# A given order for the first stage of a hybrid transformer layer: normalization, modulation and the first value projection

## The chip, the cores and the metric

The kernel runs on one core of a Trainium2 chip. The core has a matrix engine (PE), three engines for elementwise work (DVE, ACT, POOL), a queue engine that issues most of the loads and stores (SP), and 16 DMA engines that move the data. The metric is the device time of one execution in microseconds, as the median of several executions. A profile is one further execution with the hardware profiler on; its span is the time from the first to the last instruction.

## The reference

The reference is one layer of a diffusion transformer over 1024 latent tokens of width 1024, with 256 context tokens beside them. All is in float32. What matters here is its beginning:

```python
m_lat = silu(c) @ w_mod + b_mod          # 6 vectors of 1024: sh1, sc1, g1, sh2, sc2, g2
m_ctx = silu(c_ctx) @ w_mod + b_mod
h_lat = rms_norm(x, norm1_g) * (1.0 + sc1) + sh1
h_ctx = rms_norm(ctx, norm1_g) * (1.0 + csc1) + csh1
p_lat = h_lat @ w_in                     # 3584 columns: retention q, k, v, gate; attention q, k, v
p_ctx = h_ctx @ w_in
```

Behind it come a retention and a differential attention, an output projection with a gated residual, and a gated MLP with a convolution, also with a gated residual. The layer ends with a normalization.

## The kernel before

**Number format.** A float32 product is made of three products of a faster format: each operand is split into a high part (a rounded copy, on ACT) and a low part (the difference, on DVE or POOL). The function `passes` (L126) issues high times high (L129), high times low (L130) and low times high (L131) into one accumulator. Below, "product" is one such matmul with 512 columns; tile names with hi, or `hT` and `cT` as written on ACT, are high parts.

**First stage, L489 to L634.** `w_in` is cut into seven column groups of 512; the stage makes the first one, group 6 (the values of the attention), for the latent row tiles 0 to 5 of 128 rows each. The feature dimension of 1024 is cut into eight blocks of 128, called `d` or `k`. For each block the stage needs
- the modulation of this block: `mod_load` loads 128 x 2 columns of `w_mod` in two halves of 512 KB into one of five buffers `wt`; `mod_part` (L514) multiplies a half with the conditioning vectors, four small matmuls into `mods` (named `pr` in the profile); `mod_columns` (L519) copies the result to `rw` on ACT, sums it with two tiny matmuls into `pm` and writes the scale and shift columns `mcol` on DVE;
- the normalized rows: `normalize` (L528) takes the squares of a row tile on ACT, adds epsilon on DVE, takes the power -1/2 on POOL (L114 and L115) and scales the tile in place on DVE;
- the transposed and modulated block: `modulate` (L534) transposes four row tiles of 128 x 128 on PE into `pt`, applies scale and shift on ACT (high part, `hT`), does the same on DVE into `tmp`, and subtracts for the low part, on POOL where `d` is odd and on DVE where it is even. `pm` and `pt` share three banks;
- a slice of `w_in`, two blocks in a load of 512 KB (`raw`), split by ACT and DVE into `whi` and `wlo`.

`latents(0, d)` is `modulate` for row tiles 0 to 3, `latents(1, d)` for tiles 4 to 7. Row tiles 0 to 3 accumulate their products block by block in four banks (`part`) while the blocks are being made; the other half's normalization and transposes are spread between products by a generator (`second_rows`, through `beside` and `tick`), and so are the context rows (`ctx_rows`) between the products of row tiles 4 and 5. Row tiles 6 and 7 and the two context tiles follow at L649 and L650, then the other column groups.

**What sets the order.** The kernel is written against a scheduler that takes the instructions in the order of the program as a wish and gives each engine its order by its own estimate of when operands are ready. Each engine then executes strictly in that order. The function `in_order` (L117) takes a stretch of the program and chains the instructions of PE, DVE, ACT and SP to one another, so that the order written is the order executed; POOL is not chained. Before, it is used in the attention and at one place of the MLP.

Of the kernel before, what the change touches and what calls it, by code (L numbers as in the profile page):

```python
# [17 lines left out]
P = 128  # L18
# [54 lines left out]
def kernel(  # L73
# [39 lines left out]
    def rsqrt(out_ap, in_ap, mul, eps, n):  # L113
        nc.vector.tensor_scalar(out=out_ap, in0=in_ap, scalar1=mul, scalar2=eps, op0=ALU.mult, op1=ALU.add)  # L114
        nc.gpsimd.tensor_tensor(out=out_ap, in0=out_ap, in1=mhalf[:, :n], op=ALU.pow)  # L115
# [36 lines left out]
    with ExitStack() as p1:  # L152
# [344 lines left out]
        with ExitStack() as p0:  # L497
# [20 lines left out]

            def mod_columns(d):  # L519
                rw = xp.tile([P, 2 * P], F32, name="rw", bufs=2)  # L520
                nc.scalar.copy(rw, mods[:, d % 2])
                pm = pst.tile([P, 2, 2], F32, name="pm", tag="tr")
                for j in range(2):
                    mm(pm[:, j, :], rw[:, j * P : (j + 1) * P], fold, start=True, stop=True)
# [3 lines left out]
            def normalize(xt, col):  # L528
                sq = xp.tile([P, D], BF16, name="sq", bufs=1)
                nc.scalar.activation(sq, xt, AF.Square, accum_out=sm[:, col : col + 1])  # L530
                rsqrt(sm[:, col : col + 1], sm[:, col : col + 1], 1.0 / D, EPS, 1)
                nc.vector.tensor_scalar(out=xt, in0=xt, scalar1=sm[:, col : col + 1], scalar2=None, op0=ALU.mult)

# [12 lines left out]

            mods, wts = mm_tile("pr").rearrange("p (a b) -> p a b", a=2), {}
            wget, more = stream_parts(6)
            xc = []
            xs1 = [xp.tile([P, D], F32, name=f"xs1_{t}") for t in range(4)]  # L550

            def load_row(t):
# [4 lines left out]

            def part_products(t, k):
                passes(part[t], lat_lhs(t, k), wget(k, 0, 512), k == 0, k == KD - 1)
                tick()  # L560

            def second_rows():
                for t in range(4):
                    normalize(xs1[t], 6 + t)
                    yield
                for d in range(KD):
                    latents(1, d)
                    yield

            def ctx_rows():  # L570
                for t in range(NTC):
                    normalize(xc[t], t)
                    yield
                for d in range(KD):
                    modulate(xc, d, 1, cT[0][:, d, :], cT[1][:, d, :])
                    yield

            store = store_to(dv_row, c0=NTC)
            mod_load(0, 0)
            for t in range(3):  # L580
                load_row(t)
            mod_load(0, 1)
            load_row(3)
            more()
            for n in range(2, 5):
                mod_load(*divmod(n, 2))
            for q in range(2):
                mod_part(0, q)
            mod_load(2, 1)
            for t in range(4):  # L590
                normalize(xs0[t], 2 + t)
            mod_columns(0)
            latents(0, 0)
            for q in range(2):
                mod_part(1, q)
            mod_columns(1)
            latents(0, 1)
            more()
            part = [mm_tile("pn") for _ in range(4)]
            for k in range(KD):  # L600
                n = k + 2
                if k == 5:
                    beside(second_rows(), 0.9)
                if k == 6:
# [6 lines left out]
                if n + 1 < KD:  # L611
                    for q in range(2):
                        mod_load(n + 1, q)
                if k in (1, 2):
                    load_row(2 * k + 2)
                    load_row(2 * k + 3)
                if k in (1, 3):
                    more()
                part_products(0, k)
                if n < KD:  # L620
                    mod_part(n, 0)
                part_products(1, k)
                if n < KD:
                    mod_part(n, 1)
                part_products(2, k)
                if n < KD:
                    mod_columns(n)
                    latents(0, n)
                part_products(3, k)
            for t in range(4):  # L630
                store(t, part[t])
            beside(ctx_rows(), 0.7)
            natural(wget, lat_lhs, range(4, 6), store)
            beside(iter(()), 0.0)  # L634
        rc = late.enter_context(tc.tile_pool(name="rc", bufs=1))
# [817 lines left out]
```

## Time and profile before

| | |
|---|---|
| time, median of 3 executions | 1415.55 us (1414.84 to 1416.83) |
| profiled execution, its own time | 1411.45 us |
| its span | 1409.6 us |
| mean granted PE clock | 0.996 |
| PE, busy in the span | 97% |
| DVE, ACT, POOL, busy in the span | 70%, 52%, 20% |

The rows of the profile read as follows. A timeline row gives the start in the span, the duration, the engine, the line of the kernel, the operation with output and inputs, their shape, the count of instructions, and in brackets how long the engine stood idle before it and what ended that. Matmuls are pipelined, so one begins before the other ends: their pace is read from start to start, not from the duration. A float32 matmul counts as two instructions. A group of waits gives the total, the number and the longest.

### The profile page before, as it was taken

The page shows a single profiled execution, that of the slowest core. Times are in us where ns is not written, and L with a number is a line of the kernel's source. Part 1 is how long each engine was busy: PE and PEld are TensorE (multiplying, and loading weights), DVE is VectorE, ACT ScalarE, POOL GpSimd, SP SyncE. Part 2 cuts the span into 40 slices and gives each one's busy share as a digit, 9 for nine tenths or more (in the row PEclk, how much of TensorE's full clock was granted, in tenths as well). Part 3 has the DMA queues.
Part 4 walks back from the last instruction along what each step waited for, and adds up shares of the span by engine and source line. Part 5 has one row for each costly group of instructions (what it writes and reads, how often), then busy time and mean ns, then how long its engine had stood idle before and what let it go on. Part 6 is the DMA issues. An engine that isn't in the chain of part 4 may idle for free.

```text
span 1409.6 us, 19335 instructions
## 1 busy us (share of the span) xinstructions
PE 1365.5 (97%) x6988; PEld 1139.6 (81%) x6988; DVE 991.9 (70%) x1443; ACT 729.8 (52%) x1390; POOL 286.9 (20%) x321
## 2 busy tenths in 40 slices
PE   6899999999999999999999999999999999999996
PEld 3678888888887799998888778888888888788885
DVE  3564965333686798886457987777788877898457
ACT  3652312333575689997136645555455555455533
POOL 1320000000656133411201242233332220000001
PEclk9999999999999999999999999999999999999998
DMA  8535886365474697632321223223223226953224
GB/s 332 208 141 199 271 285 206 126 191 183 148 252 157 187 215 163 130 67 74 151 93 50 97 97 112 111 92 113 103 106 113 98 78 224 383 181 104 90 97 179
DMA packets 96663, 218.81 MB, mean 155 GB/s; under 512 B 9204, under 2 KB 31220, under 8 KB 96056
## 3 DMA queue, kind: packets, MB, share of 16 engines
q1 hardware_dynamic: 88408, 192.67, 39.6%
q0 software_dynamic: 8160, 24.91, 7.8%
q8 instruction: 55, 0.90, 0.3%
q14 instruction: 40, 0.33, 0.1%
HBM read 160.13 MB, written 57.41 MB: 154 GB/s over the span
## 4 chain that ended last, share of the span: by engine, by line
PE 79%; DMA 6%; issue 5%; DVE 5%; POOL 3%; ACT 2%; SPq 0%; POOLq 0%; DVEq 0%; ACTq 0%
PE chain L129 5%; PE pA L756 5%; PE chain L130 5%; PE pv L788 5%; PE chain L131 5%; PE c L131 4%; PE c L130 4%; PE c L129 4%; PE pn L130 4%; PE pn L131 3%; PE pn L129 3%; PE pl L131 3%; PE pl L129 3%; PE pl L130 3%; DMA W<-w_down 2%
## 5 line engine op out<-in xcount | busy, mean ns | idle before, releaser
L129 PE MATMUL chain<-T,whi 128*128 128x512 f32 x264 | 103.8, 394 | 5.0 <-ACT ua L1169 3.9
L129 PE MATMUL pl<-hT,whi 128*128 128x512 f32 x256 | 106.2, 415 | 0.0
L130 PE MATMUL chain<-T,whi 128*128 128x512 f32 x264 | 103.5, 392 | 0.0
L131 PE MATMUL chain<-T,wlo 128*128 128x512 f32 x264 | 103.1, 391 | 0.0
L131 PE MATMUL pl<-hT,wlo 128*128 128x512 f32 x256 | 100.2, 391 | 0.0
L130 PE MATMUL pl<-hT,whi 128*128 128x512 f32 x256 | 100.0, 391 | 0.0
L759 DVE TENSOR_REDUCE mt<-pA 128x1 f32<-128x1280 f32 x64 | 95.3, 1490 | 3.8 <-PE pA L756 2.7
L131 PE MATMUL c<-whi,ghl 128*128 128x512 f32 x232 | 90.4, 390 | 0.8 <-DVE ghl L1253 0.8
L756 PE MATMUL pA<-ks,qhl 128*128 128x512 f32 (+1 forms) x384 | 89.5, 369 | 1.0 <-ACT p L763 1.0
L130 PE MATMUL c<-wlo,ghl 128*128 128x512 f32 x232 | 90.3, 389 | 0.0
L129 PE MATMUL c<-whi,ghl 128*128 128x512 f32 x232 | 90.3, 389 | 0.0
L763 ACT ACTIVATE p<-pA,mt 128x1280 f32<-128x1280 f32 x64 | 85.5, 1336 | 6.5 <-DVE mt L759 6.5
L927 ACT CAST whi<-cmb 128x512 fp32r<-128x512 f32 x62 | 38.6, 623 | 85.1 <-PE chain L130 55.3
L129 PE MATMUL pn<-whi,hT 128*128 128x512 f32 x192 | 78.9, 412 | 1.3 <-ACT hT L541 1.0
L756 PEld LDWEIGHTS pA<-ks,qhl 128*128 128x128 f32 x384 | 67.6, 189 | 13.1 <-ACT p L763 1.7
L130 PE MATMUL pn<-wlo,hT 128*128 128x512 f32 x192 | 77.0, 401 | 0.4 <-DVE wlo L187 0.4
L1082 POOL TENSOR_TENSOR cmb<-wrb 128x512 f32<-128x512 f32 x20 | 26.4, 1322 | 249.3 <-DMA wrb<-w_up 90.4
L788 PE MATMUL pv<-va,aT 128*128 128x128 f32 x640 | 77.0, 276 | 0.1
L131 PE MATMUL pn<-whi,hT 128*128 128x512 f32 x192 | 75.7, 398 | 0.7 <-POOL hT L545 0.6
L788 PEld LDWEIGHTS pv<-va,aT 128*128 128x128 f32 x640 | 74.0, 192 | 1.0 <-DVE yT L817 0.6
L115 POOL TENSOR_TENSOR sm<-sm,mhalf 128x1 f32<-128x1 f32 x26 | 16.3, 626 | 286.2 <-DVE sm L114 286.1
L928 DVE TENSOR_TENSOR wlo<-cmb,whi 128x512 fp32r<-128x512 f32 x62 | 56.2, 908 | 21.7 <-ACT whi L927 21.3
(296 smaller groups left out, 3804.9 us busy)
## 6 DMA issues: line engine op xcount, KB each, us to landing
wm<-w_mod SPq DMA_DIRECT2D x32, 512.0 KB, 5.2
raw<-w_in SPq DMA_DIRECT2D x28, 512.0 KB, 5.1
wra<-w_up SPq DMA_DIRECT2D x24, 512.0 KB, 3.4
wrb<-w_up SPq DMA_DIRECT2D x23, 512.0 KB, 3.6
W<-w_down SPq DMA_DIRECT2D x44, 256.0 KB, 5.8
ad<-s SPq DMA_DIRECT2D x20, 512.0 KB, 3.5
wra<-ad SPq DMA_DIRECT2D x20, 512.0 KB, 3.3
kvs<-kvg SPq DMA_DIRECT2D x36, 256.0 KB, 3.0
```

Of the source, the lines that this page charges most:

```text
L115: nc.gpsimd.tensor_tensor(out=out_ap, in0=out_ap, in1=mhalf[:, :n], op=ALU.pow)
L129: mm(ps, lh, rh, start=first, stop=False, skip_group_check=more)
L130: mm(ps, lh, rl, start=False, stop=False, skip_group_check=more)
L131: mm(ps, ll, rh, start=False, stop=last, skip_group_check=more)
L756: mm(self.pa[m][:, c0:c1], self.q[:, m, i, qs], self.k[:, m, c0:c1], start=(i == 0), stop=(i == 1))
L759: nc.vector.tensor_reduce(out=self.mt[:, m : m + 1], in_=self.pa[m][:, :LK], axis=AX.X, op=ALU.min)
L763: nc.scalar.activation(self.p[m], self.pa[m][:, :LK], AF.Exp, scale=-1.0, bias=self.mt[:, m : m + 1], accum_out=self.s[:, m : m + 1])
L788: mm(self.pv, self.aT[:, c, :], self.v[:, c, :], start=(c == 0), stop=(c == NKT - 1))
L927: nc.scalar.copy(hi, src)
L928: nc.vector.tensor_tensor(out=lo, in0=src, in1=r32(hi), op=ALU.subtract)
L1082: nc.gpsimd.tensor_tensor(out=s1, in0=b1, in1=b2, op=ALU.add)
```

## The change

The stage is rewritten as one explicit sequence from the first load to the store of row tile 5, and `in_order` fixes it on PE, DVE, ACT and SP. Within it, the helper functions are cut into their steps (`mod_row` and `mod_sums` for `mod_columns`; `square`, `power` and `scale` for `normalize`), each of which has a place of its own. Each feature block has one batch of transposes, of sums and of modulation matmuls between its products. The first weight slice is loaded and split in two halves. Twenty matmuls of a tile of ones (`turn_over`) are added at the beginning; their result is overwritten. The generators are gone: squares and scaling of the second half stand in blocks 3 to 5, its transposes in blocks 6 and 7 and in row tile 4, and the context rows in row tiles 4 and 5. The diff, cut to what matters:

```diff
-            def mod_columns(d):
-                rw = xp.tile([P, 2 * P], F32, name="rw", bufs=2)
-                nc.scalar.copy(rw, mods[:, d % 2])
+            def mod_row(d):
+                rws[d] = xp.tile([P, 2 * P], F32, name="rw", bufs=2)
+                nc.scalar.copy(rws[d], mods[:, d % 2])
+            def mod_sums(d):
+                rw = rws.pop(d)
...
+            def scale(xt, col, c0=0, c1=D):
+                nc.vector.tensor_scalar(out=xt[:, c0:c1], in0=xt[:, c0:c1], scalar1=sm[:, col : col + 1], scalar2=None, op0=ALU.mult)
...
+            def part_products(ts, k):
+                for t in ts:
+                    passes(part[t], lat_lhs(t, k), wget(k, 0, 512), k == 0, k == KD - 1)
+            def turn_over(n):
+                for _ in range(n):
+                    mm(part[3][:, :P], ones, ones, start=True, stop=True)
...
+            turn_over(4)
+            mod_part(0, 0)
+            turn_over(10)
...
+            scale(xs0[3], 5, 0, 2 * P)
             latents(0, 0)
+            mod_part(1, 0)
+            mod_part(1, 1)
+            mod_row(1)
...
             for k in range(KD):
+                part_products((0, 1), k)
+                if k == 0:
+                    mod_sums(1)
+                    latents(0, 1)
+                if k < 2:
+                    for q in range(2):
+                        mod_part(k + 2, q)
+                    mod_row(k + 2)
+                if k == 7:
+                    latents(1, 2)
+                    latents(1, 3)
+                if 1 < k < 6:
+                    load_row(k + 2)
+                n = k + 4
+                if n < KD:
+                    for q in range(2):
+                        mod_load(n, q)
+                if k in (0, 2):
+                    w_load(2 + k // 2)
+                part_products((2, 3), k)
+                if k + 2 < KD:
+                    mod_sums(k + 2)
+                    latents(0, k + 2)
+                    if 0 < k < 5:
+                        for q in range(2):
+                            mod_part(k + 3, q)
+                        mod_row(k + 3)
+                if k in (0, 2, 4):
+                    w_split()
+                if k == 3:
+                    square(xs1[0], 6)
+                    power(6)
+                if k == 4:
+                    square(xs1[1], 7)
+                    scale(xs1[0], 6)
+                    power(7)
                 if k == 5:
...
+                    square(xs1[2], 8)
+                    scale(xs1[1], 7)
+                    power(8)
+                    square(xs1[3], 9)
+                    scale(xs1[2], 8)
+                    power(9)
+                    scale(xs1[3], 9)
+                if k >= 6:
+                    latents(1, 4 * (k - 6))
+                    latents(1, 4 * (k - 6) + 1)
...
+            def between(t, k):
+                if (t, k) == (4, 0):
+                    latents(1, 6)
+                    latents(1, 7)
...
+                if t == 5 and k % 2:
+                    context(k - 1)
+                    context(k)
...
+            in_order(begin)
```

How this moves the instructions is shown at three places. In the rows, `xs_172` to `xs_175` are the row tiles 0 to 3, and `xs_0` to `xs_3` with a number behind are the row tiles 4 to 7; `hT_168` and `hT_170` are high and low part of the first half, `hT_169` and `hT_171` of the second.

PE at the beginning of the program, before:

```order
L517 MATMUL pr<-wt,cz 32x256 x8
L524 MATMUL pm<-fold,rw 128x2 x2
L538 MATMUL pt<-ident,xs_172 128x128
L538 MATMUL pt<-ident,xs_173 128x128
L538 MATMUL pt<-ident,xs_174 128x128
L538 MATMUL pt<-ident,xs_175 128x128
L517 MATMUL pr<-wt,cz 32x256 x4
L129 MATMUL pn<-whi,hT_168 128x512
L130 MATMUL pn<-wlo,hT_168 128x512
```

and with the change:

```order
L590 MATMUL pn<-ones 128x128 x4
L517 MATMUL pr<-wt,cz 32x256 x4
L590 MATMUL pn<-ones 128x128 x10
L517 MATMUL pr<-wt,cz 32x256 x4
L590 MATMUL pn<-ones 128x128 x2
L527 MATMUL pm<-fold,rw 128x2 x2
L590 MATMUL pn<-ones 128x128 x4
L545 MATMUL pt<-ident,xs_172 128x128
```

The matmuls of ones (L590) fill the places between the first modulation matmuls, the sums and the transposes.

PE within feature block 1, before, from one half of a modulation batch to the products behind the transposes:

```order
L517 MATMUL pr<-wt,cz 32x256 x4
L130 MATMUL pn<-wlo,hT_168 128x512
L131 MATMUL pn<-whi,hT_170 128x512
L129 MATMUL pn<-whi,hT_168 128x512
L524 MATMUL pm<-fold,rw 128x2 x2
L538 MATMUL pt<-ident,xs_172 128x128
L538 MATMUL pt<-ident,xs_173 128x128
L538 MATMUL pt<-ident,xs_174 128x128
L538 MATMUL pt<-ident,xs_175 128x128
L130 MATMUL pn<-wlo,hT_168 128x512
```

and in a block with the change:

```order
L131 MATMUL pn<-whi,hT_170 128x512
L527 MATMUL pm<-fold,rw 128x2 x2
L545 MATMUL pt<-ident,xs_172 128x128
L545 MATMUL pt<-ident,xs_173 128x128
L545 MATMUL pt<-ident,xs_174 128x128
L545 MATMUL pt<-ident,xs_175 128x128
L517 MATMUL pr<-wt,cz 32x256 x8
L129 MATMUL pn<-whi,hT_168 128x512
```

The two halves of a modulation batch, which had products between them, now stand together behind the transposes.

ACT before, around the squares of the last two latent row tiles:

```order
L521 COPY rw<-pr 128x256
L530 ACTIVATE sq,sm<-xs_2_201 128x1024
L541 ACTIVATE hT_168<-pt,mcol 128x512
L530 ACTIVATE sq,sm<-xs_3_202 128x1024
L521 COPY rw<-pr 128x256
L186 CAST whi<-raw 128x1024
```

and with the change, at the end of block 5:

```order
L533 ACTIVATE sq,sm<-xs_1_204 128x1024
L548 ACTIVATE hT_168<-pt,mcol 128x512
L533 ACTIVATE sq,sm<-xs_2_205 128x1024
L533 ACTIVATE sq,sm<-xs_3_206 128x1024
L548 ACTIVATE hT_169<-pt,mcol 128x512 x4
L186 CAST whi<-raw 128x1024
```

The two squares stood ahead of the high parts of blocks 6 and 7 before; now they stand behind the first half's last high part (block 7), directly ahead of the second half's high parts.

POOL before, up to the context rows:

```order
L115 TENSOR_TENSOR sm<-sm,mhalf 128x1 x3
L545 TENSOR_TENSOR hT_170<-tmp,hT_168 128x512
L115 TENSOR_TENSOR sm<-sm,mhalf 128x1 x2
L545 TENSOR_TENSOR hT_170<-tmp,hT_168 128x512
L545 TENSOR_TENSOR hT_171<-tmp,hT_169 128x512
```

and with the change:

```order
L552 TENSOR_TENSOR hT_170<-tmp,hT_168 128x512 x3
L115 TENSOR_TENSOR sm<-sm,mhalf 128x1 x2
L552 TENSOR_TENSOR hT_170<-tmp,hT_168 128x512
L115 TENSOR_TENSOR sm<-sm,mhalf 128x1 x2
L552 TENSOR_TENSOR hT_171<-tmp,hT_169 128x512 x4
```

The powers (L115) of row tiles 6 and 7 are now behind the low part of block 7. Behind the stage the engines' rows are the same as before, except that on SP two loads and stores have changed places, and that a weight split of the next column group (ACT L186, DVE L187) stands within the transposes of the second half on ACT and DVE, in both versions.

More of the change, by code (lines that the diff above doesn't have):

```diff
@@ L545, in modulate, with wget, w_load, w_split @@
                 eng.tensor_tensor(out=lo, in0=tmp[:, :n], in1=r32(hi), op=ALU.subtract)
-            mods, wts = mm_tile("pr").rearrange("p (a b) -> p a b", a=2), {}
-            wget, more = stream_parts(6)
-            xc = []
+            mods, wts, rws = mm_tile("pr").rearrange("p (a b) -> p a b", a=2), {}, {}
+            part = [mm_tile("pn") for _ in range(4)]
+            sl, raws, xc = [], [], []
             xs1 = [xp.tile([P, D], F32, name=f"xs1_{t}") for t in range(4)]
+            def wget(k, c0, c1):
+                return tuple(t[:, k % 2, c0:c1] for t in sl[k // 2])
+            def w_load(kk, n=1):
+                raws.append(wr.tile([P, 2, 512], F32, name="raw"))
+                for i in range(0, 2, 2 // n):
+                    nc.sync.dma_start(out=raws[-1][:, i : i + 2 // n], in_=w_in[6][:, 2 * kk + i : 2 * kk + i + 2 // n, :])
+            def w_split(i0=0, i1=2):
+                if i0 == 0:
+                    sl.append(tuple(wp.tile([P, 2, 512], F32R, name=nm) for nm in ("whi", "wlo")))
+                hi, lo = (t[:, i0:i1] for t in sl[-1])
+                raw = raws[len(sl) - 1][:, i0:i1]
+                nc.scalar.copy(hi, raw)
+                nc.vector.tensor_tensor(out=lo, in0=raw, in1=r32(hi), op=ALU.subtract)
             def load_row(t):
@@ L599 @@
-            part = [mm_tile("pn") for _ in range(4)]
-            for k in range(KD):
-                n = k + 2
+                mod_load(1, q)
+            mod_load(2, 0)
+            turn_over(4)
+            mod_part(0, 0)
+            turn_over(10)
+            square(xs0[0], 2)
+            square(xs0[1], 3)
+            power(2)
+            power(3)
+            scale(xs0[0], 2)
+            square(xs0[2], 4)
+            mod_part(0, 1)
+            mod_load(2, 1)
+            w_load(1)
```

93 lines of the change are left out of this document (37 added, 56 removed).

## The prediction

> **What bounds the kernel now.** I read the page first, then the busy time by stretches, then PE's waits, then PE row by row up to the first product of row tile 6.
>
> ```profile
> PE 1365.5 (97%) x6988; PEld 1139.6 (81%) x6988; DVE 991.9 (70%) x1443; ACT 729.8 (52%) x1390; POOL 286.9 (20%) x321
> ```
>
> PE is the bound of the whole: whatever it waits less here comes off the end, unless a later wait is tied to something that doesn't move. The stretches, each with length, busy time of PE, PEld, DVE, ACT and POOL, clock, DMA share and GB/s:
>
> ```profile
> 7.00:17.70 10.70, 5.15 (x32) 2.03 (x31) 4.91 (x12) 6.60 (x11) 2.21 (x4) 1.00 1.03 421
> 17.70:82.06 64.36, 59.51 (x357) 39.64 (x354) 36.62 (x65) 30.84 (x51) 17.83 (x17) 1.00 0.59 220
> 82.06:1409.60 1327.54, 1300.73 (x6605) 1097.83 (x6603) 949.33 (x1357) 690.84 (x1327) 266.38 (x295) 1.00 0.47 150
> ```
>
> The change ends where row tile 6 begins, which PE's rows put at 82.06: the row ahead of it is tile 5's last product.
>
> ```profile
> 81.82 0.40 PE L131 MATMUL pn<-whi,hT 128*128 128x512 f32 x1
> 82.06 0.39 PE L129 MATMUL pn<-whi,hT 128*128 128x512 f32 x1
> ```
>
> From 17.70 to there PE is idle for 64.36 - 59.51 = 4.85 us. That is the first thing to win. The second is in the pace of the products, start to start:
>
> ```profile
> 11.79 1.08 PE L517 MATMUL pr<-wt,cz 128*32 128x256 f32 x8 [3.82 <-DMA wt<-w_mod]
> ...
> 16.35 0.48 PE L538 MATMUL pt<-ident,xs 128*128 128x128 f32 x1 [1.24 <-DVE xs L532]
> ...
> 18.79 0.63 PE L129 MATMUL pn<-whi,hT 128*128 128x512 f32 x1
> 19.22 0.63 PE L130 MATMUL pn<-wlo,hT 128*128 128x512 f32 x1
> ...
> 23.36 0.64 PE L517 MATMUL pr<-wt,cz 128*32 128x256 f32 x8
> ```
>
> A product takes 0.43 us at 19 us and 0.24 at 82; the same half of a modulation batch takes 1.08 us at 11.8 and 0.64 at 23.4. So half pace ends between 19.6 and 23.4, by the rows between at about 22.4, some 6 us after PE last stood still (16.35). The third is the price of switching between kinds of matmul:
>
> ```profile
> 30.98 0.39 PE L129 MATMUL pn<-whi,hT 128*128 128x512 f32 x1
> 31.30 0.64 PE L517 MATMUL pr<-wt,cz 128*32 128x256 f32 x8
> 31.87 0.50 PE L131 MATMUL pn<-whi,hT 128*128 128x512 f32 x1
> 32.21 0.39 PE L130 MATMUL pn<-wlo,hT 128*128 128x512 f32 x1
> ...
> 33.04 0.63 PE L538 MATMUL pt<-ident,xs 128*128 128x128 f32 x4
> 33.60 0.64 PE L517 MATMUL pr<-wt,cz 128*32 128x256 f32 x8
> ...
> 36.67 0.50 PE L524 MATMUL pm<-fold,rw 128*128 128x2 f32 x4
> 37.03 0.64 PE L538 MATMUL pt<-ident,xs 128*128 128x128 f32 x4
> 37.42 0.47 PE L130 MATMUL pn<-wlo,hT 128*128 128x512 f32 x1
> 37.73 0.39 PE L131 MATMUL pn<-whi,hT 128*128 128x512 f32 x1
> ...
> 78.61 0.38 PE L538 MATMUL pt<-ident,xc 128*128 128x128 f32 x2
> 78.75 0.48 PE L129 MATMUL pn<-whi,hT 128*128 128x512 f32 x1
> ```
>
> From start to start: half a modulation batch (pr) 0.57, with 0.09 more for the product before it and 0.11 for the one after; the sums (pm) 0.36; four transposes 0.39, with 0.08 on the product behind, or 0.56 where a pr follows; two context transposes 0.14.
>
> **The start.** In the new order the first batch of transposes still waits for row tile 3, whose load stands at the same place of SP's queue, and behind it come the same three steps: high part on ACT, scaled copy and low part on DVE. So block 0's low part is ready at about the same time. These are DVE's rows (the first shows the copy waiting for ACT's high part):
>
> ```profile
> 18.52 0.69 DVE L545 TENSOR_TENSOR hT<-tmp,hT 128x512 fp32r<-128x512 f32 x1
> ...
> 34.60 0.81 DVE L543 TENSOR_SCALAR tmp<-pt,mcol 128x512 f32<-128x512 f32 x1 [0.98 <-ACT hT L541]
> 37.53 0.14 DVE L114 TENSOR_SCALAR sm<-sm 128x1 f32<-128x1 f32 x1
> 38.34 0.75 DVE L532 TENSOR_SCALAR xs<-xs,sm 128x1024 f32<-128x1024 f32 x1 [0.66 <-POOL sm L115]
> ```
>
> Before, it is ready at 18.52 + 0.69 = 19.2; I take 19.0, since half a weight split moves behind it. Before, PE had fitted high-part products into this gap; now the third product waits, for 0.9 us. The 20 dummy products (L590) stand where PE waits anyway, for a load or for row tile 3, and keep it at work without a break from 6.9 to about 14 us, longer than those 6 us. So the products start at 0.23. If the dummies did nothing for the pace, 16.5 to 22.4 would run at half pace as before; PE would finish block 0 1.9 us later (a pr pair and the first block's products at twice the time, less the 0.9 of waiting that they fill); if they raised it earlier still, nothing more is won, since the chain to 19.0 is ACT's and DVE's. I take the full pace.
>
> **The blocks.** With the low part there at 19.0:
> - block 0: 12 products less the two already done 2.3, pm and transposes 0.36 + 0.56 + 0.36 + 0.47, two pr 1.14, two switches: 5.8, to 24.8;
> - block 1: 12 x 0.23 = 2.8, two double pr 2.3, pm and transposes 0.9, switches 0.3: 6.3, to 31.1;
> - blocks 2 to 4: 2.8 + 0.36 + 0.56 + 1.14 + 0.11 = 4.95 each, to 45.9;
> - block 5: 2.8 + 0.36 + 0.39 + 0.08 = 3.6, to 49.5; block 6: 2.8, to 52.3.
>
> All other work of these blocks lies beside PE: per block ACT has a high part, a row copy and a weight split or square, DVE a copy, a low part, at times a weight split and a scaling (0.81 + 0.69 + 1.22 + 0.75 by rows here and below), both under 4.95. The loads must be ahead, which is the third rival.
>
> **A new wait.** Squares of row tiles 6 and 7 now stand behind block 7's high part on ACT, and their powers behind block 7's low part on POOL; the new transposes of the second half need all four tiles.
>
> ```profile
> 33.72 0.78 ACT L541 ACTIVATE hT<-pt,mcol 128x512 fp32r<-128x512 f32 x1 [1.28 <-PE pt L538]
> ...
> 38.39 1.05 ACT L530 ACTIVATE sq<-xs 128x1024 bf16<-128x1024 f32 x1
> ```
> ```profile
> 35.49 1.28 POOL L545 TENSOR_TENSOR hT<-tmp,hT 128x512 fp32r<-128x512 f32 x1 [9.04 <-DVE tmp L543]
> 37.75 0.55 POOL L115 TENSOR_TENSOR sm<-sm,mhalf 128x1 f32<-128x1 f32 x1 [0.97 <-DVE sm L114]
> ```
>
> From 49.5: high part 0.78, copy 0.81, to 51.1; the scaling of tile 5 (0.75) first, to 51.8; POOL's low part 1.28, to 53.1; its power 0.55, to 53.7; tile 6 scaled 0.75, to 54.4; then DVE's sum, POOL's power and back 0.81 (37.53 to 38.34) and tile 7 scaled 0.75: 56.0. PE has finished block 6 at 52.3 and, in fixed order, can't go on to block 7: **3.6 us of wait** (less the last transposes). ACT's squares (2 x 1.1 behind 50.3) are done at 52.5, so POOL and DVE set it. Before, tile 7 was scaled long before its transposes, so this wait did not exist:
>
> ```profile
> 50.48 0.75 DVE L532 TENSOR_SCALAR xs<-xs,sm 128x1024 f32<-128x1024 f32 x1 [1.84 <-POOL sm L115]
> ```
> ```profile
> 57.32 1.07 PE L538 MATMUL pt<-ident,xs 128*128 128x128 f32 x8
> ```
>
>
> **To the end of tile 5**, from 56.0: block 7 and its transposes in batches of four and eight, 0.4 + 1.47 + 0.8 + 1.47 + 0.8 = 5.0, to 61.0; tile 4's first three products 0.8 and one batch 0.4, to 62.2. The next batch needs a transpose bank that DVE's copy of block 4 frees, and a weight split for the next column group stands ahead of that copy. What such an operation costs while POOL works:
>
> ```profile
> 65.71 1.68 POOL L545 TENSOR_TENSOR hT<-tmp,hT 128x512 fp32r<-128x512 f32 x1 [1.14 <-DVE tmp L543]
> ```
> ```profile
> 66.15 1.79 DVE L532 TENSOR_SCALAR xc<-xc,sm 128x1024 f32<-128x1024 f32 x1
> ...
> 69.90 2.31 DVE L187 TENSOR_TENSOR wlo<-raw,whi 128x1024 fp32r<-128x1024 f32 x1
> ```
>
> and without it:
>
> ```profile
> 41.65 1.22 DVE L187 TENSOR_TENSOR wlo<-raw,whi 128x1024 fp32r<-128x1024 f32 x1
> ```
>
> DVE's copies and low parts, counted from 56.0 with 0.75 and 0.65 each, reach the split at 61.2. It ends at 62.4 by the short row and 63.5 by the long one, the copy at 63.2 or 64.3; I take the middle, a wait of 1.7. [...] From 63.9: the batch 0.4, the other 21 products of tile 4 4.95, to 69.3; six products 1.4, to 70.7. The context rows' powers on POOL stand behind block 7's low part of the second half: copied on DVE by 67.4, 1.68 on POOL to 69.1, power 0.6, two scalings 0.75 each, 71.3, a wait of 0.6. Then 18 products 4.2 and four context batches 0.36 each, to 76.95.
>
> **The sum.** 82.06 - 76.95 = 5.1 us less. By sources: idle 4.85 before against 0.9 + 3.6 + 1.7 + 0.6 = 6.8 now, so the waits themselves grow; the half pace after 17.7 gives 2.3 back; the rest, about 4.8, is fewer switches and work done before the start. Behind 82 us each engine's rows keep their order but for two loads and stores exchanged, and PE's 27 us of idle time there hang on rows that move with PE, so I take all of it to the end: 1411.45 - 5.1 = 1406.3 for the profiled execution. The median shown is 4.1 us above that execution, which gives **1410.4**.
>
> **Rivals.** (1) *Half pace comes back in the new wait.* From 52.3 to 56.0 PE has only three transposes. Against it: the one longer pause in the rows (3.82 ahead of 11.79) came at half pace already, so no row shows it. [...] The mechanism's price from rows: as at the start, 6 us at half pace, up to 3 us, 2.6 with the waits that it fills. That gives about 1413.
> (2) *No such waits*: POOL's low part and the split cost nothing. Then 3.6 + 1.7 + 0.6 fall away and it is 1404.5. Against it: the order of ACT and POOL is fixed there.
> (3) *The load loop becomes the bound*, the slower side. A w_mod half is loaded into one of five buffers, when a matmul five halves before has freed it.
>
> ```profile
> SPq L511 <- PE pr L517: 20.4, 8, 5.7
> ```
> ```profile
> DMA to landing us min/median/max: 3.9/8.0/10.0
> ```
>
> By the first row (total, times, longest) SP already waits 20.4 us for such buffers; by the second a load takes 8.0 us from issue to landing in the median, 10.0 at most. In the new order the second half of block 5 is issued at about 27 and needed at 35, others alike: 8 us. With the median the loads come just in time; each us above it is lost twice before block 7. At 10.0 four us are lost, at 10.6 all, at 12 it is slower by 2.9 (1418.4). Against it: the 8.0 is mostly a queue of loads at 421 GB/s, and a block asks 1.8 MB in 4.95 us, 371 GB/s.
> (4) *Given back later*: some load behind 82 us lands as late as before, and the end stays at about 1415. For it only that a few PE waits there are for DMA.
>
> **How the numbers follow.** The forecast has a chance of 0.62, rival (1) 0.12, (2) 0.10, (3) 0.08, (4) 0.08. The unknown terms within the forecast (1.9 for the early pace, 1.1 for the split, up to 3 for landings) make it 1407 to 1413.5; with (1) and part of (2) and (4) the range is 1406.5 to 1414.5. About 0.2% (2.8 us) is what can be told from no change here: faster by more 0.74, within 0.18, slower 0.08.
>
> **What would show it.** Tile 6's first product near 77 us; products at 0.23 from the first one; PE's longest wait ahead of the second half's first transposes, 3 to 4 us, ended by DVE's scaling; a wait of 1 to 2 us in tile 4 for the copy. Wrong it is if PE waits for w_mod after block 1, or if the products behind that pause run at 0.43.

## The result, and the profile after

The changed kernel takes 1409.18 us (median of 6 runs, 1407.05 to 1411.80) against 1414.71 us for the kernel before (6 runs beside it). The ratio is 0.9962, with a 95% interval of 0.9947 to 0.9976, so it is faster. In two later comparisons on other occasions the same kernel came to 0.9984 [0.9974, 0.9993] and 0.9970 [0.9960, 0.9980]. By the medians the three gains are 5.5, 2.2 and 3.8 us; over all three the gain is about 0.3%, or 4 us. The profiled execution took 1407.91 us.

The page of the changed kernel has the same bound, PE, and nearly the same work: the 20 dummy matmuls of ones count as 40 instructions, and the operations that were cut in halves make two more on DVE and one on ACT:

```profile
PE 1366.5 (97%) x7028; PEld 1147.6 (82%) x7028; DVE 991.4 (71%) x1445; ACT 729.6 (52%) x1391; POOL 287.5 (20%) x321
```

The stretch that held 64.36 us before (17.70 to 82.06) now holds 59.65. The columns are length, busy time of PE, PEld, DVE, ACT and POOL, clock, DMA share and GB/s:

```profile
17.70:77.35 59.65, 54.60 (x351) 41.43 (x344) 35.73 (x65) 30.35 (x50) 16.55 (x16) 0.97 0.63 238
```

PE's idle time in it is 59.65 - 54.60 = 5.05 us, much the same as the 4.85 before. So the gain isn't in the waits but in PE's busy time, 59.51 before and 54.60 here. PE's rows, in order of time, show where it is:

```profile
6.98 1.08 PE L517 MATMUL pr<-wt,cz 128*32 128x256 f32 x8 [3.71 <-DMA wt<-w_mod]
...
12.23 0.64 PE L517 MATMUL pr<-wt,cz 128*32 128x256 f32 x8 [0.62 <-DMA wt<-w_mod]
...
19.04 0.50 PE L131 MATMUL pn<-whi,hT 128*128 128x512 f32 x1 [0.43 <-DVE hT L552]
19.37 0.40 PE L129 MATMUL pn<-whi,hT 128*128 128x512 f32 x1
...
51.02 0.38 PE L545 MATMUL pt<-ident,xs 128*128 128x128 f32 x2
53.24 0.33 PE L545 MATMUL pt<-ident,xs 128*128 128x128 f32 x1 [1.83 <-DVE sm L114]
54.72 1.33 PE L545 MATMUL pt<-ident,xs 128*128 128x128 f32 x5 [1.16 <-DVE xs L539]
...
56.27 0.63 PE L130 MATMUL pn<-wlo,hT 128*128 128x512 f32 x1
56.70 0.63 PE L131 MATMUL pn<-whi,hT 128*128 128x512 f32 x1
...
58.30 1.04 PE L545 MATMUL pt<-ident,xs 128*128 128x128 f32 x8
...
63.92 0.66 PE L545 MATMUL pt<-ident,xs 128*128 128x128 f32 x4 [1.18 <-DVE tmp L550]
...
69.60 0.50 PE L131 MATMUL pn<-whi,hT 128*128 128x512 f32 x1 [0.45 <-POOL hT L552]
```

Three things are to be seen. At 12.23 half a modulation batch already takes 0.64 us, where it took 1.08 before: full pace is there early. Block 6 ends at 51.02. Then come two waits of 1.83 and 1.16 us for the scaled row tiles, and behind them the products start 0.43 us apart again (56.27, 56.70): half pace has come back, which was rival (1). The stage ends near 77.3 us, where 76.95 was forecast.

To compare kernels, I use the first product of the first context tile, a little behind the stage and the same instruction in all. It is called the mark below. It is at 92.95 us before and here:

```profile
88.27 0.39 PE L129 MATMUL pn<-whi,cT 128*128 128x512 f32 x1
```

That is 4.68 us earlier. At the end of the execution, however, only 3.5 are left (spans of 1409.6 and 1406.1).

### The profile page after: what moved, and what is told of

Its sections match the earlier page's. It is cut to its first block, busy times and chain, and to the rows that moved or that the text cites. A ratio compares the mean times of both kernels' runs of the same rounds, so it can differ in the third digit from the quotient of the medians.

```text
span 1406.1 us, 19426 instructions
## 1 busy us (share of the span) xinstructions
PE 1366.5 (97%) x7028; PEld 1147.6 (82%) x7028; DVE 991.4 (71%) x1445; ACT 729.6 (52%) x1391; POOL 287.5 (20%) x321
## 4 chain that ended last, share of the span: by engine, by line
PE 81%; issue 5%; DMA 5%; DVE 4%; ACT 2%; POOL 2%; SPq 0%; POOLq 0%; ACTq 0%; DVEq 0%
PE pv L869 5%; PE chain L129 5%; PE pA L837 5%; PE chain L131 5%; PE chain L130 5%; PE c L131 4%; PE c L129 4%; PE c L130 4%; PE pn L129 4%; PE pn L131 4%; PE pn L130 3%; PE pl L129 3%; PE pl L131 3%; PE pl L130 3%; PE third L129 2%
## 5 line engine op out<-in xcount | busy, mean ns | idle before, releaser
L115 POOL TENSOR_TENSOR sm<-sm,mhalf 128x1 f32<-128x1 f32 x26 | 17.0, 657 | 274.0 <-DVE sm L114 273.9
```

## The experiments

All of them are the changed kernel with one edit, except where said. The ratio is to the kernel before, measured in the same comparison.

| run | mark, us | median, us | ratio, 95% interval |
|---|---|---|---|
| before (profile) | 92.95 | | |
| changed | 88.27 | 1409.18 | 0.9962 [0.9947, 0.9976] |
| again: changed | 88.09 | 1409.02 | 0.9984 [0.9974, 0.9993] |
| e1_no_ones | 90.49 | 1411.06 | 1.0005 [0.9990, 1.0019] |
| e2_squares_early | 83.94 | 1404.25 | 0.9949 [0.9937, 0.9962] |
| e3_filled_wait | 87.46 | 1407.62 | 0.9977 [0.9968, 0.9987] |
| again2: changed | 87.54 | 1409.51 | 0.9970 [0.9960, 0.9980] |
| control: before | 93.32 | 1413.34 | 1.0008 [0.9998, 1.0017] |
| e4_free_order | 91.98 | 1414.85 | 1.0011 [1.0001, 1.0021] |
| e6_early_and_late_split | 83.63 | 1405.16 | 0.9946 [0.9932, 0.9959] |
| e7_spare_buffer | 88.11 | 1407.60 | 0.9966 [0.9953, 0.9978] |
| e8_early_and_spare | 87.21 | 1403.66 | 0.9939 [0.9925, 0.9952] |
| e9_before_spare: before | 93.76 | 1411.63 | 0.9996 [0.9987, 1.0005] |
| e5_split_batches | 90.03 | 1408.74 | 0.9980 [0.9971, 0.9989] |

The runs from again to e3, from again2 to e6 and from e7 to e5 are three comparisons on three chips: medians compare within one of them, ratios across. The mark is of one profiled execution each, and differs by up to 0.7 us between executions of one kernel (88.27, 88.09, 87.54). Part of that is the start, which hangs on the landing of the first loads: the third product of block 0 starts at 19.04, 18.97 and 19.46 in these three. Counted from it, the mark is 69.23, 69.12 and 68.08 us behind; the third is shorter for a reason of its own (half pace, below). Where two executions of full pace at the start are compared, I give this distance too: 65.10 with the squares early, 67.97 with the filled wait, 64.06 with early squares and late split, 69.29 with the spare buffer.

### The dummy matmuls

```diff
-            turn_over(4)
```
(and all other calls, 20 matmuls in all)

> As the changed kernel, without its twenty matmuls of ones. Theory A (they are what lets the first products run at full pace): modulation halves at 1.08 and products at 0.43 until about 22 us, block 0 ends 1.9 us later and the mark is at about 90.2. Theory B (the early work is enough by itself, or the pace rises at a time of its own): products at 0.23 from 19 us on and the mark at 88.3.

PE's rows without them:

```profile
12.28 1.08 PE L517 MATMUL pr<-wt,cz 128*32 128x256 f32 x8 [4.17 <-DMA wt<-w_mod]
...
20.34 0.63 PE L130 MATMUL pn<-wlo,hT 128*128 128x512 f32 x1
20.77 0.63 PE L131 MATMUL pn<-whi,hT 128*128 128x512 f32 x1
...
24.77 0.39 PE L130 MATMUL pn<-wlo,hT 128*128 128x512 f32 x1
```

The first block's products are 0.43 apart, until about 22.5 us as before the change. The mark comes 2.4 us later than in the run of the changed kernel beside it, and the time is 2.0 us longer. I had worked out 1.9, all of it from modulation matmuls and products at half pace. In the rows only half comes that way. The last transpose of block 0 starts 1.28 us later (17.48 against 16.20 in the run beside it), because the modulation sums run at half pace too (0.87 us from start to start, 0.47 in the first profile of the changed kernel) and DVE does the scalings of row tiles 2 and 3 behind the columns that it makes of them; the rest, 1.2 us up to block 1, is PE's own pace. So by the mark about half of the gain (2.4 of 4.9) is the pace of the first 22 us. The rest of the change without it shows in the mark (90.49 against 92.95) but is not told apart from the kernel before by time (1.0005).

### The wait for the scaled row tiles

Two kernels attack it. The first makes the squares and powers of row tiles 5 to 7 one block earlier, puts the last two scalings ahead of block 7's transposes, and loads row tile 7 one block earlier; a dependence keeps the next column group's weight split where it stands in the changed kernel (the diff is condensed):

```diff
 k == 3:  square(xs1[0]); power(6)
+         square(xs1[1]); scale(xs1[0]); power(7)
 k == 4:
-         square(xs1[1]); scale(xs1[0]); power(7)
+         square(xs1[2]); scale(xs1[1]); power(8); square(xs1[3]); power(9)
 k == 5:
-         square(xs1[2]); scale(xs1[1]); power(8); square(xs1[3]); scale(xs1[2]); power(9); scale(xs1[3])
+         scale(xs1[2]); scale(xs1[3])
```

> The squares, powers and scalings of row tiles 5 to 7 stand one block earlier, so that they are done before block 6 ends. Theory A (the wait ahead of the second half's transposes comes from the place of these steps, and the half pace behind it from the wait): the wait of 3.5 us falls to under 0.5, the products behind it run at 0.23 instead of 0.43 from the first one (1.6 us more), the mark comes at about 83.2, 5 us earlier than in the changed kernel, and the time is some 5 us lower. Theory B (the next scarce thing, the three transpose banks and DVE's copies, takes the place of the wait): the mark moves by less than 2.5 us and the waits for DVE's copy in tile 4 grow by as much.

```profile
50.86 1.03 PE L549 MATMUL pt<-ident,xs 128*128 128x128 f32 x8
...
59.11 0.66 PE L549 MATMUL pt<-ident,xs 128*128 128x128 f32 x4 [1.20 <-DVE tmp L554]
```

All eight transposes run without a wait (no bracket in the first row). The mark is 4.15 us earlier than in the changed kernel beside it (4.02 counted from the third product) and the time 4.8 us shorter (1404.25 against 1409.02). The wait and the half pace behind it together are worth about 4 us, and putting them right nearly doubles the gain of the change.

The second fills the wait with 14 matmuls of ones and leaves the wait itself:

```diff
+                if k == 6:
+                    for _ in range(14):
+                        mm(mods[:, 0, :P], ones, ones, start=True, stop=True)
```

> As the changed kernel, with 14 matmuls of ones between block 6 and the second half's transposes, where PE waits 3.5 us for the scaled rows; their result is not used. Theory A (half pace returns because PE stands still): the wait's end stays at 54.7, but the products behind it start 0.23 apart and the mark comes 1.6 us earlier, at 86.7. Theory B (the slow products have another reason, such as operands or POOL and DVE at work beside them): still 0.43 apart and the mark at 88.3 or later.

```profile
51.49 3.29 PE L687 MATMUL pr<-ones 128*128 128x128 f32 x28
54.62 1.35 PE L545 MATMUL pt<-ident,xs 128*128 128x128 f32 x8
...
56.27 0.40 PE L131 MATMUL pn<-whi,hT 128*128 128x512 f32 x1
56.51 0.39 PE L129 MATMUL pn<-whi,hT 128*128 128x512 f32 x1
```

The products behind are 0.24 apart instead of 0.43. One profile would not settle it, since the pause goes unpunished in one of the six that have it; but none of the four without it (the filled wait and the three with early squares) has half pace there, so it comes of PE's standing still, Theory A. Its price is best read from another execution of the changed kernel (again2), in which the same pause brought no half pace:

```profile
55.19 0.76 PE L545 MATMUL pt<-ident,xs 128*128 128x128 f32 x5 [1.15 <-DVE xs L539]
...
57.17 1.04 PE L545 MATMUL pt<-ident,xs 128*128 128x128 f32 x8
```

Five transposes and six products take 1.98 us there and 3.58 in the first profile (54.72 to 58.30): 1.6 us, as expected. From those transposes to the mark it is 32.35 against 33.55 us, so **1.2 us** are left there; the three waits behind come to 1.84 us instead of 1.63. The mark with the filled wait came only 0.6 to 0.8 us earlier (expected 1.6), but its execution had also started later, with the third product at 19.49. Counted from it, the mark is 1.2 us earlier (67.97 against 69.23 and 69.12), and the time fell by 1.4, though with intervals that overlap.

### The order itself, and the batches

```diff
-            in_order(begin)
```

> The changed kernel with its new sequence of instructions, but without the last line that fixes it on the engines, so the scheduler orders PE, DVE, ACT and SP by its own estimate. Theory A (the gain comes from what stands where in the rows, above all one batch per block and full pace from the start, and the scheduler undoes part of it): both halves of a modulation batch stand apart again, PE's waits for copies and low parts return, the mark comes at 89 to 91. Theory B (the sequence and the matmuls of ones are enough): the mark at 88 or earlier, since PE may go on to block 7 while it would wait for the scaled rows.

The mark is at 91.98, and the time is that of the kernel before or up to 0.2% longer. That is later than either theory had, and the rows say why:

```profile
1.19 5.06 PE L590 MATMUL pn<-ones 128*128 128x128 f32 x22 [1.19 <-DVE ones L111]
...
7.31 2.27 PE L590 MATMUL pn<-ones 128*128 128x128 f32 x18
11.56 0.64 PE L517 MATMUL pr<-wt,cz 128*32 128x256 f32 x8 [1.98 <-DMA wt<-w_mod]
...
17.25 0.63 PE L130 MATMUL pn<-wlo,hT 128*128 128x512 f32 x1
```

Without the fixed order the scheduler puts the ones earlier (11 and 9 matmuls, none behind the second modulation half), and PE then stands still for 1.98, 0.49, 1.24 and 0.87 us. The clock that was granted is 0.50 from 13.7 to 20.5, and the products run at half pace in it (0.43 from the start at 19.41 us to the next at 19.84). So this run changes two things at once: its 3.7 us at the mark hold both the loss of pace and the batches that the scheduler takes apart again. For the batches alone, one half is put between the products of row tile 2 and those of row tile 3:

```diff
-                part_products((2, 3), k)
+                part_products((2,), k)
+                if 0 < k < 5:
+                    mod_part(k + 3, 0)
+                part_products((3,), k)
...
-                        for q in range(2):
-                            mod_part(k + 3, q)
+                        mod_part(k + 3, 1)
```

> The changed kernel with the modulation matmuls of blocks 1 to 4 in two halves again, one of them between the two pairs of products, as the kernel before had them. Theory A (a batch costs two switches, 0.2 us in all, wherever it stands): blocks 1 to 4 take 0.2 us more each, the first context product comes 0.8 us later, near 88.8, and the time rises by 0.8 us, ratio to before about 0.9975. Rival (batching is worth nothing, because the block's chain over DVE and ACT sets its length): blocks keep 4.8 us and the product stays at 88.0.

PE's rows of block 2 in this kernel, up to the first product of block 3:

```profile
31.61 0.50 PE L129 MATMUL pn<-whi,hT 128*128 128x512 f32 x1
...
33.91 0.64 PE L517 MATMUL pr<-wt,cz 128*32 128x256 f32 x8
34.48 0.50 PE L129 MATMUL pn<-whi,hT 128*128 128x512 f32 x1
...
36.21 0.64 PE L517 MATMUL pr<-wt,cz 128*32 128x256 f32 x8
36.78 0.50 PE L129 MATMUL pn<-whi,hT 128*128 128x512 f32 x1
```

and of the changed kernel:

```profile
30.23 0.50 PE L129 MATMUL pn<-whi,hT 128*128 128x512 f32 x1
...
34.01 1.07 PE L517 MATMUL pr<-wt,cz 128*32 128x256 f32 x16
35.01 0.50 PE L129 MATMUL pn<-whi,hT 128*128 128x512 f32 x1
```

A block takes 5.17 us with the batch in two, 4.78 with it in one: 0.39 us, twice what I had expected for two switches. Two halves in a row take 1.00 (34.01 to 35.01) and not 2 x 0.57; that is the other part. Over blocks 1 to 4 it makes 1.5 us. The mark of 90.03 isn't this alone: block 0 ended 1.0 us later in this profile, with a late modulation load and half pace, and the bank wait in row tile 4 fell from 1.18 to 0.16. By the ratio the time is 1.1 us above the mean of the changed kernel's three, but its interval overlaps each of theirs, so the time doesn't show it. The rival (batching is worth nothing) is refuted by the rows.

### The bank wait

The squares early, and the weight split held back by one block more (the diff is against the kernel with the squares early):

```diff
                     latents(1, 3)
-                    held_back.append(last DVE instruction)
...
                     latents(1, 4 * (k - 6))
+                    if k == 7:
+                        held_back.append(last DVE instruction)
```

> Squares early as in the second experiment, which came out at 83.9 at the mark and 1404.25 us, and the next column group's weight split on DVE behind the copy of block 4 of the second half instead of ahead of it. Theory A (the wait of 1.2 us in row tile 4 is for that copy, which waits behind the split): the wait falls to under 0.3, the mark to about 82.9, the time 1 us lower. Theory B (the wait is for ACT's high part or for the bank anyway): the wait stays at 1 us or more and the mark at 83.9.

The wait for DVE's copy is gone (1.20 us to none); for POOL's low parts there are two waits (0.31, 0.52) instead of one (0.46). The mark is only 0.3 us earlier than with the squares early alone, but this execution started 0.73 later (third product at 19.57 against 18.84): counted from there, the mark is 64.06 us behind instead of 65.10, the 1 us of Theory A. The time doesn't show it (0.9946 against 0.9949).

### Where the rest of the gain goes

Two more comparisons of the changed kernel, and one of the kernel before with itself, each with a profile:

> The changed kernel once more, unchanged. The mark for the end of the stage is the start of the first product of the context tiles: 92.95 us before, 88.27 in the changed kernel, 4.7 us earlier, of which only 3.5 us are left at the end of the two profiled executions. Theory A (all of it goes to the end, the missing 1.2 us are chance of two executions): the mark again at 88.3 within 0.3, the ratio near 0.9965. Theory B (about 1 us is given back behind the stage each time): the mark the same, the span again only some 3.5 us under the one before, a ratio near 0.9975.

> The kernel before, as a run of its own, beside the shared runs of the same kernel: it gives a second profile of it. Theory A (what the second comparison lacks, 2.2 us at the end for 4.9 us at the mark, is chance of the executions): the stages behind the mark last as differently from one profile of this kernel to the next as from before to after, 1 to 2 us each, with no one stage always shorter; ratio 1.000 within 0.001. Theory B (the changed kernel really gives back 1 to 2 us behind the stage): in this profile too the retention and attention stages together are some 2 us shorter than in both profiles of the changed kernel.

> The changed kernel a third time, on the same chip as the control. Theory A: ratio near 0.9965, the mark at 88.2. Theory B: ratio near 0.998 once more, the mark at 88.2.

From the mark to the last products the kernel before took 1304.6 us in one profile and 1310.8 in the other, so a difference of one pair of profiles there says little, and why the changed kernel's ratios differ as they do (0.9962, 0.9984, 0.9970) stays open. One loss, though, is in all three profiles of the changed kernel: PE waits 2.7, 2.6 and 2.4 us for ACT's exponentials in the attention, against 1.0 and 1.2 before. DVE's rows for the rotation there, of the kernel before:

```profile
465.29 0.69 DVE L417 SCALAR_TENSOR_TENSOR xa<-pl,rtab 128x512 f32<-128x512 f32 x1 [2.10 <-ACT xb L415]
...
477.47 0.68 DVE L418 TENSOR_TENSOR xb<-xb,rtab 128x512 f32<-128x512 f32 x1
```

and with the change:

```profile
461.27 0.69 DVE L417 SCALAR_TENSOR_TENSOR xa<-pl,rtab 128x512 f32<-128x512 f32 x1 [2.10 <-ACT xb L415]
...
475.16 0.68 DVE L418 TENSOR_TENSOR xb<-xb,rtab 128x512 f32<-128x512 f32 x1
```

The lead falls from 4.02 to 2.31 us within twelve. Between them ACT stands:

```profile
467.10 0.62 ACT L407 CAST xhl<-xa 128x512 fp32r<-128x512 f32 x1 [1.69 <-DMA dq<-xhl]
```

The split of a query (L407) has two buffers. This one needs the buffer of the split before the last, whose store `dq` was issued at 453.80 and lands 13.2 us later, with the DMA engines busy throughout (a share of 1.1 to 1.2 between 455 and 470 us). ACT's exponentials and DVE's reductions are queued behind that cast, and PE waits 1.71 us, until 471.40, for such an exponential. In the kernel before the same cast starts at 469.40 without a wait; its store had been issued at 457.26 and landed 12.0 us later. So the store came 3.5 us earlier with the change, the landing only 2.3. Three kernels test it, with a tile that is unused there as a third buffer for this one split:

```diff
-            hl = ev.tile([P, 2, 512], F32R, name="xhl")
+            hl = spare.pop() if spare else ev.tile([P, 2, 512], F32R, name="xhl")
...
-        alpad.tile([P, 1024], F32, name="alpad", bufs=1)
+        spare.append(alpad.tile([P, 2, 512], F32R, name="alpad", bufs=1))
```

> The changed kernel, with one more buffer for the first query split after the attention's score matmuls have begun (the cast of xhl, L407, which waited 1.7 us for the store dq of an older split at 467 us). Theory A (the stage's gain is given back in part there: 4.7 us at the first context product, 4.0 at 465 us, 2.3 from 477 us on): that wait of ACT goes to 0, PE's wait for the exponentials (pA for ACT p) falls from 2.7 us to about 1.0, the stretch from the first to the last score matmul shortens from 190.1 to about 188.8 us, and the time falls by 1.3 to 1.7 us against the changed kernel: ratio to before about 0.9960. Theory B (the buffer wait only covers another late transfer, so PE waits as long for qhl, ks or va): the same stretch stays near 190 and the time near that of the changed kernel, ratio about 0.9970. The first context product stays at 88 us by both.

> The kernel before with the same spare buffer alone. Theory A: in its two profiles that cast waited 0 and 0.6 us and PE at most 0.3 us for it, so the time changes by 0 to -0.3 us (ratio 0.9998 to 1.0000) and the stretch of the score matmuls stays at 188.7. Rival: the buffer helps every version alike, by 1.3 us (ratio 0.9991), and then the loss at this place is not of the change's making.

> Squares early as in the earlier run, plus the spare buffer for the query split. Theory A: the two gains add up, since the wait of the attention was 2.9 us with the squares early: first context product near 84.0 us, wait of pA for ACT p about 1.0, time 1.5 to 2 us below the run with the squares early alone, ratio to before about 0.9935. Theory B: 0.9949 as there.

ACT's row of the cast and DVE's of the rotation, in the changed kernel with the third buffer:

```profile
465.54 0.61 ACT L407 CAST alpad<-xa 128x512 fp32r<-128x512 f32 x1
```
```profile
461.50 0.69 DVE L417 SCALAR_TENSOR_TENSOR xa<-pl,rtab 128x512 f32<-128x512 f32 x1 [2.10 <-ACT xb L415]
...
473.59 0.68 DVE L418 TENSOR_TENSOR xb<-xb,rtab 128x512 f32<-128x512 f32 x1
```

The cast no longer waits, the lead is 3.79 us ahead of the place and 3.88 behind it, and PE's wait for the exponentials is 1.0. From the first to the last score matmul it takes 188.2 us (190.1 without the buffer, 188.7 before). So Theory A is shown in the trace: 1.7 us are lost at this one buffer. The ratios don't resolve it (0.9966 against 0.9962 to 0.9984). In the kernel before, the buffer changes nothing in the time that can be measured (0.9996), as Theory A had it, though its stretch of score matmuls also gets 0.6 us shorter (188.1); so of the 1.9 us that the buffer takes off the stretch in the changed kernel, some 1.3 are of the change's making. Together with the early squares it gives 0.9939, the lowest ratio of all versions, though its interval overlaps that of the early squares alone. The mark of the two together, 87.21 against 83.94 without the buffer, belongs to one profiled execution, in which half pace came back at the start (below). The early squares alone are clearly faster than the changed kernel beside them (0.9949 against 0.9984).

## Why the prediction was right

The forecast was 1410.4 us in a range of 1406.5 to 1414.5; it took 1409.18. The sum came out at 5.1 us for the stage, and 4.7 to 4.8 were measured. The single steps were off by more, in both directions, so that the sum fits is in part luck; and so is the time, since the stage's 4.7 us came with gains of 5.5, 2.2 and 3.8 us in the three comparisons.

- **The start and full pace**: 19.04 for the third product, forecast 19.0; it waited 0.43 instead of 0.9. The dummies do what was said, and the price agrees (2.0 measured, 1.9 worked out), but half of it came through DVE's scalings, which I had not counted. (In the DVE rows that I showed there, it is the second, not the first, that waits for ACT's high part.)
- **The blocks**: block 6 ended at 51.02, forecast 52.3. The term that was mis-sized most is the double batch, 1.00 us instead of 1.14: six of them make 0.8 of the 1.3 us, and blocks 2 to 4 take 4.78 us each, not 4.95. The terms that I listed for block 0 also add up to at most 5.6, not 5.8; it took 5.21.
- **The new wait** was there, with its cause: POOL's low part of block 7, then two powers, each followed by a scaling on DVE, as DVE's rows show:

```profile
52.43 0.75 DVE L539 TENSOR_SCALAR xs<-xs,sm 128x1024 f32<-128x1024 f32 x1 [1.61 <-POOL sm L115]
...
53.91 0.75 DVE L539 TENSOR_SCALAR xs<-xs,sm 128x1024 f32<-128x1024 f32 x1 [0.67 <-POOL sm L115]
```

  From the end of block 6 (51.02) to the last tile's transposes (54.72) it took 3.7 us, forecast 3.6, and PE stood still for 2.99 of it. The run with early squares takes it away.
- **Half pace after it** was the rival that I gave 0.12, and it is what happened, in this profile and in four of the five others that have the same pause. The prediction itself named products at 0.43 behind that pause as a sign that it is wrong, so the forecast, which took full pace there, failed at this step. I had given it the price of 2.6 us, from 6 us at half pace; it lasted 3.4, and costs 1.6 on the six products and 1.2 at the mark. The faster blocks (1.3 us) paid for it, by luck: without half pace the stage would have ended near 76.2.
- **The bank wait** was 1.18 us, forecast 1.7. These are the rows of DVE and of POOL:

```profile
61.93 1.22 DVE L187 TENSOR_TENSOR wlo<-raw,whi 128x1024 fp32r<-128x1024 f32 x1
```
```profile
58.38 1.28 POOL L552 TENSOR_TENSOR hT<-tmp,hT 128x512 fp32r<-128x512 f32 x1 [4.51 <-DVE tmp L550]
62.09 2.18 POOL L552 TENSOR_TENSOR hT<-tmp,hT 128x512 fp32r<-128x512 f32 x1 [2.42 <-DVE tmp L550]
```

  The split took its short time, 1.22, and POOL's low part, which started 0.16 later, took 2.18 instead of 1.28. I had taken the middle of the short and the long row; by the short row alone, 0.55 us less, the wait comes to 1.15. The rows of the kernel before show DVE slow beside POOL (1.79 against 0.75); here POOL was the slow one.
- **A wait not foreseen**: 0.45 us at 69.60 for POOL's low part. POOL itself had stood idle for 1.35 us until DVE's copy came; on DVE, two low parts beside POOL's had taken 0.92 and 1.17 us instead of 0.69. The context wait (0.6) didn't come.
- **Rival (3)**: PE waits for `w_mod` nowhere behind block 0 in this profile. In three of the nine profiles with this start (again, the early squares with the buffer, the batches in two) block 1's second half came 0.32, 0.45 and 0.64 us late. The loads are just in time, as the median said, but don't bound the blocks.
- **Rival (4)** had 0.08, and a third of it is true: 1.3 to 1.7 us are given back, not at a load but at a store.

## What to carry to other kernels

When a stage is moved ahead, look along its whole lead for the first instruction that waits on something that does not move with it; here one two-buffer tile took back up to 1.7 of 4.7 us, and comparing the same instructions in both traces found it. A pause of PE can cost more than its length: here 3.4 us of half pace came behind waits of 3 us together in five of six profiles. Price that too, and prefer to move the producers of its operands (4 us here) to filling it (1.4 us). In a fixed order, put together what is of one kind: a pair of modulation halves back to back saved 0.39 us a block.

## What the runs showed of the hardware

Where the clock's column shows half pace within the stage, it lasted 3.4 or 6.8 us. The clock granted in the changed kernel, in stretches of 1 us (third number from the right):

```profile
54.00:55.00 1.00, 0.28 (x2) 0.28 (x3) 0.67 (x1) 0.00 (x0) 0.00 (x0) 0.86 0.00 0
55.00:56.00 1.00, 1.00 (x6) 1.00 (x6) 0.00 (x0) 0.77 (x1) 0.00 (x0) 0.50 0.00 0
...
58.00:59.00 1.00, 1.00 (x9) 0.90 (x8) 0.30 (x1) 0.07 (x1) 0.62 (x1) 0.93 0.07 16
```

and in another profile of the same kernel (again2), whose pause has the same rows (1.84 and 1.15 us):

```profile
54.00:55.00 1.00, 0.03 (x1) 0.00 (x0) 0.62 (x1) 0.00 (x0) 0.34 (x1) 1.00 0.00 0
55.00:56.00 1.00, 0.81 (x6) 0.80 (x7) 0.13 (x1) 0.45 (x1) 0.00 (x0) 1.00 0.00 0
```

In the first the clock is at one half for 2 x 0.14 + 3 + 2 x 0.07 = 3.4 us; in the second it never drops. Summed in the same way, it is 3.4 us in all five profiles in which this pause brought it (of six that have the pause), 3.4 at the start of the run with split batches, and 6.8, twice that, at 13.7 to 20.5 us of the run with free order. Where it begins differs: with the transposes that end the pause in the first (54.72), 0.8 us behind them in the profile of the run again (55.46 against 54.66). At the start of the run with early squares and buffer it is 6.8 again, behind pauses of only 1.14 and 0.45 us:

```profile
17.00:19.00 2.00, 1.55 (x18) 0.46 (x10) 1.33 (x2) 1.09 (x3) 0.00 (x0) 0.92 1.03 424
...
23.00:25.00 2.00, 2.00 (x17) 0.73 (x14) 0.81 (x1) 0.83 (x2) 0.36 (x1) 0.50 0.22 80
25.00:27.00 2.00, 2.00 (x11) 1.70 (x11) 0.00 (x0) 0.26 (x1) 0.91 (x1) 0.88 0.85 248
```

So a pause isn't punished each time: the same pause (in one of them 0.2 us longer) brought half pace in five of six profiles, and what decides it isn't shown. Nor did PE have to stand still for as long as the half pace lasts: in the 3.4 us before the drop at 18.7 us in the run with early squares and buffer, its longest pause was 1.14 us, and modulation matmuls ran at 16.71 and 17.80 us. How much work it takes to keep full pace was not measured. At the start of the kernel before, the clock's column shows 1.00 while products run at 0.43, so there only the pace tells it.
